# First half-FFN: ten pairs of the input phase by seven block products, modulation fetched one condition at a time in order of need, the context's operand at the memory's other end

## The chip, the core and the metric

The kernel runs on one core of a Trainium2 chip. The metric is the device time of one execution in microseconds (us); the profile is one execution recorded by the hardware profiler. Five engines matter: TensorE does the matmuls (PE; its weight loads, PEld, overlap them), VectorE (DVE) and ScalarE (ACT) prepare operands and finish results, GpSimd (POOL) does little here, and SyncE (SP) issues nearly all transfers, in order, on one queue. Each engine works through its own list of instructions in order; one that waits on a semaphore holds up everything behind it on that engine.

## The reference, cut to what matters

```python
def modulation(cond, w_mod, b_mod):
    m = jax.nn.silu(cond) @ w_mod + b_mod
    return m.reshape(m.shape[:-1] + (N_MOD, D_MODEL))          # 9 rows of 1024

def modulate(x, m, k):
    return x * (1 + m[..., 3 * k + 1, :]) + m[..., 3 * k, :]

def post_norm_update(x, y, m, k, g, b):
    return layer_norm(DN_ALPHA * x + m[..., 3 * k + 2, :] * y, g, b)

def swiglu(h, w_in, w_out):
    gate, up = jnp.split(h @ w_in, 2, axis=-1)
    return (jax.nn.silu(gate) * up) @ w_out

def macaron_half_ffn(x, m, k, w_in, w_out, g, b):
    return post_norm_update(x, 0.5 * swiglu(modulate(x, m, k), w_in, w_out), m, k, g, b)

# two layers; x is 512 tokens of 1024, ctx 256 tokens of 1024, the hidden width is 2816
for i in range(DEPTH):
    mx = modulation(c, mod_w[i], mod_b[i])
    x = macaron_half_ffn(x, mx, 0, ...)
    if ctx_needed:                                             # layer 0 only
        mc = modulation(c_ctx, mod_w[i], mod_b[i])
        ctx = macaron_half_ffn(ctx, mc, 0, ...)
    ...                                # mixer (HGRN2 or chunk MLP), then a second half-FFN
```

All of it is float32.

## The kernel before

**A product of float32 matrices** is made of three matmuls. Every operand is split into a high part (a rounded copy, by ACT, L135) and a low part (the difference, by DVE, L136), and `mm3` issues high times high, high times low and low times high (L148, L149, L150) into one PSUM bank. A *unit* is one weight tile of 128 x 1024 (512 KB): SP issues its load into `raw` (L141, a ring of three buffers), ACT writes the high half of `w` and DVE the low half (a ring of six), and PE uses it in eight steps of 128 rows.

**The first half-FFN on x** (`f0`, a `FeedIn`) needs gate and up for 22 hidden tiles, so 44 units in 22 *pairs*. The first three pairs (six units, `nu=6`) are fed while x arrives: for each of the eight row blocks k, DVE makes two columns of modulation (scale and shift) as dot products of rows of `mod_w` with the row silu(c), ACT applies them (L1014, L1019 for k = 0), the result is split into the operand `xm` (512 tokens), and `products` gives PE whatever that k allows. Then `rest(hp, 2)` (L590) does the other 19 pairs plainly: 2 units x 8 steps x 3 matmuls of 128x512, after which `evac` makes silu (ACT, L580) and h (DVE, L582). The out phase on x (`y`, 22 units of 24 matmuls of 128x512) follows, then the same weights once more for the 256 context tokens (`f1`, matmuls of 128x256, `psf<-xmc` in the rows), then the context's out phase. While `f1` runs, DVE and SP also finish x: the layer norm's last two steps (L338, L339) and the stores of x (L340).

**Modulation.** Beyond the two columns of the start, a `mod_task` makes one row of 1024: eight loads of 512 KB (`mraw`, two buffers, L176), each followed by dots with the silu row of one condition or of both (`x`, `c`). A dot is two instructions on halves of 512 (L170, each with its read of the accumulator) and, at the end of a row, a reduction joins the halves (L183). `mod_step(n)` takes the next n loads of the queue, with fractions saved up; it is called after each pair or unit. The queue holds: rows 2, 4, 3 for both conditions on one load, rows 1 and 0 for c, then 5, 7, 6, 8 and the next layer's row 2 for x: 80 loads and 104 dots.

**Seven products.** The second half-FFN of layer 0 and both of layer 1 already use another form of a pair (`seven`, of class `Forms`): gate and up together are a product of blocks, 2 x 2 blocks of the operand (halves of the 1024 rows, halves of the 512 tokens) by 2 x 2 blocks of the weights, done with seven block products in place of eight (Strassen-Winograd). The blocks of x are summed once (`sum_steps`: f5, f6, f7, f4); for every pair DVE makes three sums of weights (L660 to L663), so two loads become three and a half split weights. A pair is then 84 matmuls of 128x256 (`psc`, `pse`, `psa`). Its results leave through ACT (`sc`, L726) and DVE (L770 to L780).

**What sets the order.** The program names instructions in the order that one reads; a scheduler, with its own estimate of durations, then decides each engine's list, keeping what `issue_after` ties (a mod step behind the latest split). Buffers are tiles of pools: a tile that is used again makes the writer wait for its last reader.

**Memory.** The context's operand `xmc` (16 KB per partition, pool `xcp`) is taken from the start on the left side and kept until L1368, so the startup and `f0` do not have that space.

## Time and profile before

| | |
|---|---|
| three runs of the kernel | 2445.36, 2445.84, 2446.22 us; median 2445.84 |
| the profiled execution | 2444.88 us |
| its span in the profile | 2443.2 us |
| granted TensorE clock | 0.999 of full speed |

The stages, by the first and last starts of their matmuls in the trace:

| stage | us from the span's start | form of the matmuls |
|---|---|---|
| startup: three pairs while x arrives | 10.6 to 52 | 128x512 |
| 19 plain pairs of `f0` | 52 to 258 | 128x512 |
| out phase of x | 259 to 378 | 128x512 |
| input phase of the context, `f1` | 379 to 508 | 128x256 |
| out phase of the context, then HGRN2 | 508 to 1008 | mixed |
| second half-FFN of layer 0, input phase (seven products) | from 1009 | 128x256 |

How to read what follows: a row of the timeline is start, duration, engine, line, operation, what it writes and reads; the interval between the starts of two neighbours is what an instruction costs its engine, and that is often less than its duration, since neighbours overlap. A row of the windows gives, for a stretch of time, the busy time of each engine with its count, the granted clock, the mean share of the DMA engines in use and the bytes per second. "Idle before" and the arrow name what ended an engine's wait.

### The profile page before, as it was taken

How to read it: one execution, taken by the hardware profiler on the slowest of the kernel's cores; microseconds unless marked ns; L12 is line 12 of the kernel's file. 1: busy time of each engine (PE TensorE's matmuls, PEld its weight loads, DVE VectorE, ACT ScalarE, POOL GpSimd, SP SyncE). 2: the span in 40 equal slices, each digit the busy share in tenths (PEclk: the TensorE clock that was granted, in tenths of full speed). 3: DMA queues.
4: the chain of work that ended last, by engine and by line, in shares of the span. 5: the costliest groups of instructions: out<-in, count | busy, mean ns of one | idle time of the engine just before them, and what ended most of it. 6: DMA issues, size and time to landing. Idle time of an engine off the chain costs nothing.

```text
span 2443.2 us, 38143 instructions
## 1 busy us (share of the span) xinstructions
PE 2412.5 (99%) x14907; PEld 2186.0 (89%) x14907; DVE 1960.8 (80%) x3532; ACT 1151.1 (47%) x1784; POOL 35.2 (1%) x57
## 2 busy tenths in 40 slices
PE   7999999999999999999999999999999999999998
PEld 5888889988888888999988999988999988999987
DVE  7965679786488886988796988898898787988785
ACT  4222334454454452555643555544654443555641
POOL 0000000000000000000000000000000000000000
PEclk9999999999999999999999999999999999999999
DMA  8866555874212113433474333574322365333452
GB/s 325 296 207 203 164 177 193 297 245 162 67 48 65 61 48 113 160 104 106 147 235 151 104 104 104 163 248 154 115 86 99 116 226 170 130 114 104 139 163 79
DMA packets 107430, 366.01 MB, mean 150 GB/s; under 512 B 12473, under 2 KB 13809, under 8 KB 107249
## 3 DMA queue, kind: packets, MB, share of 16 engines
q1 hardware_dynamic: 107248, 363.58, 44.6%
q8 instruction: 116, 1.90, 0.3%
q14 instruction: 66, 0.53, 0.1%
HBM read 350.92 MB, written 12.61 MB: 149 GB/s over the span
## 4 chain that ended last, share of the span: by engine, by line
PE 89%; DVE 6%; ACT 3%; issue 1%; DMA 1%; POOL 0%; SPq 0%; DVEq 0%; POOLq 0%; ACTq 0%
PE y L148 10%; PE y L150 10%; PE y L149 10%; PE psf L150 5%; PE psf L149 5%; PE psf L148 5%; PE psc L148 5%; PE psc L150 5%; PE psc L149 5%; PE pse L150 3%; PE pse L148 3%; PE pse L149 3%; PE psa L150 1%; PE psa L149 1%; PE psa L148 1%; PE psq L148 1%
## 5 line engine op out<-in xcount | busy, mean ns | idle before, releaser
L136 DVE TENSOR_TENSOR w<-raw,w 128x1024 fp32r<-128x1024 f32 (+3 forms) x447 | 501.1, 1126 | 158.3 <-ACT w L135 157.4
L135 ACT ACTIVATE w<-raw 128x1024 fp32r<-128x1024 f32 (+3 forms) x447 | 436.1, 978 | 389.7 <-DMA raw<-in_ffn_w_in 71.4
L148 PE MATMUL y<-w,hs 128*128 128x512 f32 x984 | 383.7, 390 | 0.0
L150 PE MATMUL y<-w,hs 128*128 128x512 f32 x984 | 383.1, 389 | 0.0
L149 PE MATMUL y<-w,hs 128*128 128x512 f32 x984 | 382.9, 389 | 0.0
L135 ACT ACTIVATE hs<-h 128x512 fp32r<-128x512 f32 (+1 forms) x220 | 126.1, 587 | 202.1 <-PE y L150 180.4
L150 PEld LDWEIGHTS y<-w,hs 128*128 128x128 f32 x984 | 184.6, 188 | 39.7 <-DVE hs L136 1.3
L148 PEld LDWEIGHTS y<-w,hs 128*128 128x128 f32 x984 | 184.7, 188 | 38.6
L149 PEld LDWEIGHTS y<-w,hs 128*128 128x128 f32 x984 | 184.7, 188 | 37.8
L148 PE MATMUL psf<-xm,w 128*128 128x512 f32 (+1 forms) x544 | 191.3, 356 | 14.1 <-ACT xm L1019 10.6
L150 PE MATMUL psf<-xm,w 128*128 128x512 f32 (+1 forms) x544 | 192.2, 354 | 1.4 <-DVE w L136 1.4
L149 PE MATMUL psf<-xm,w 128*128 128x512 f32 (+1 forms) x544 | 192.1, 354 | 0.4 <-DVE xm L136 0.4
L136 DVE TENSOR_TENSOR hs<-h,hs 128x512 fp32r<-128x512 f32 (+1 forms) x220 | 135.3, 635 | 69.3 <-ACT hs L135 69.1
L148 PE MATMUL psc<-f,w 128*128 128x256 f32 x544 | 154.5, 284 | 1.1 <-ACT sc L726 1.1
L150 PE MATMUL pse<-f,w 128*128 128x256 f32 x544 | 154.2, 284 | 0.0
L148 PE MATMUL pse<-f,w 128*128 128x256 f32 x544 | 154.0, 283 | 0.0
L150 PE MATMUL psc<-f,w 128*128 128x256 f32 x544 | 153.9, 283 | 0.0
L149 PE MATMUL psc<-f,w 128*128 128x256 f32 x544 | 153.9, 283 | 0.0
L149 PE MATMUL pse<-f,w 128*128 128x256 f32 x544 | 153.9, 283 | 0.0
L148 PE MATMUL psc<-xm,w 128*128 128x256 f32 x532 | 151.5, 285 | 0.6 <-ACT sc L726 0.6
L150 PE MATMUL psc<-xm,w 128*128 128x256 f32 x532 | 150.5, 283 | 0.0
L149 PE MATMUL psc<-xm,w 128*128 128x256 f32 x532 | 150.5, 283 | 0.0
(342 smaller groups left out, 6013.0 us busy)
## 6 DMA issues: line engine op xcount, KB each, us to landing
raw<-in_ffn_w_in SPq DMA_DIRECT2D x159, 512.0 KB, 4.6
raw<-in_ffn_w_out SPq DMA_DIRECT2D x110, 512.0 KB, 4.2
mraw<-in_mod_w SPq DMA_DIRECT2D x80, 512.0 KB, 4.4
rawu<-in_mod_w SPq DMA_DIRECT2D x64, 512.0 KB, 4.0
rawu<-in_ffn_w_in SPq DMA_DIRECT2D x60, 512.0 KB, 3.6
x<-x SPq DMA_DIRECT2D x36, 512.0 KB, 4.4
raw<-in_hg_wf SPq DMA_DIRECT2D x32, 512.0 KB, 3.6
raw<-in_cm_w_out SPq DMA_DIRECT2D x24, 512.0 KB, 4.6
```

Of the source, the lines that this page charges most:

```text
L135: latest_hi[0] = nc.scalar.activation(dst_hi, src, AF.Copy)
L136: latest[0] = nc.vector.tensor_tensor(dst_lo, src, dst_hi.bitcast(F32), ALU.subtract)
L148: nc.tensor.matmul(ps, ah, bh, start=start, stop=False, **kw)
L149: nc.tensor.matmul(ps, ah, bl, start=False, stop=False, **kw)
L150: return nc.tensor.matmul(ps, al, bh, start=False, stop=stop, **kw)
```

## The change

Five things change.

1. `f0` becomes a `FeedSums` (still with six units in the startup). In the startup ACT also copies each modulated block of x into eight block tiles, two copies of 128x256 per k, that lie where later h tiles will be. `rest` does nine plain pairs first, one step of the sums in each of the first four, and then ten pairs by seven products.
2. A modulation row is made for one condition at a time, in order of need: 13 rows, so 104 loads of 512 KB in place of 80. The number of dots is the same. After a plain pair of `f0` 3.5 loads are taken, after a seven pair 0.5, after a unit of x's out phase 1.4 (1 before), after a pair of the context's input phase 1.4 (0.5 before).
3. A dot is one instruction over 1024 in place of two over 512, and the reduction goes. In the startup, where the accumulator has two columns, a dot is still two halves. The scratch output `junk` has one buffer in place of two.
4. `xcp` is allocated on the right side, after `f0` is done, and freed when the out phase of HGRN2 no longer needs it.
5. The modulation of the second layer, made in space cut from buffers of other stages (`Scraps`), takes one or two columns of accumulator, by the space that there is.

```diff
     def mod_dot(pool, dst, w, s):
-        n = D // 2
-        for i in range(2):
+        n = D // dst.shape[1]
+        for i in range(dst.shape[1]):
             c = slice(i * n, (i + 1) * n)
-            junk = pool.tile([P, n], BF16, tag="junk", name="junk", bufs=2)
+            junk = pool.tile([P, D // parts_of(pool)], BF16, tag="junk", name="junk", bufs=1)[:, :n]
             nc.vector.scalar_tensor_tensor(junk, w[:, c], 1.0, s[:, c], ALU.mult, ALU.mult, dst[:, i : i + 1])
+    def parts_of(pool):
+        return getattr(pool, "parts", 1)
     def mod_task(modp, srow, l, ch, conds):
-        accs = {c: modp.tile([P, KD, 2], F32, tag=f"acc_{c}", name=f"acc_{c}", bufs=2) for c in conds}
+        accs = {c: modp.tile([P, KD, parts_of(modp)], F32, tag=f"acc_{c}", name=f"acc_{c}", bufs=2) for c in conds}
...
-            dot = modp.tile([P, KD], F32, tag="dot", name="dot", bufs=2)
-            nc.vector.reduce_sum(dot, accs[c], axis=AX.X)
+            dot = accs[c][:, :, 0]
+            for i in range(1, parts_of(modp)):
+                nc.vector.tensor_tensor(dot, dot, accs[c][:, :, i], ALU.add)
...
-        def rest(self, hp, sp, nmod=0):
+        def rest(self, hp, sp, nmod=0, plain=0, nmod_plain=0):
...
-            for f in range(first, NF):
+            for f in range(first, first + plain):
+                self.plain_pair(hp, f)
+                with tc.issue_after(latest[0].ins):
+                    next(self.steps, None)
+                mod_step(nmod_plain)
+            for f in range(first + plain, NF):
...
-    xcp = L0.enter_context(sbuf(name="xcp", bufs=1))
-    xmc = new_xm(xcp, "xmc", TC)
...
-        f0 = FeedIn(0, 0, xm, NT, 6)
+        f0 = FeedSums(0, 0, xm, NT, lambda i: hp.tile([P, T], F32, tag="h", name="h", bufs=NF).rearrange("p (k t) -> p k t", k=2))
+        f0.nu = 6
...
+                for p in range(2):
+                    b = f0.blocks[p, k // 2] if k % 2 else f0.block(p, k // 2)
+                    nc.scalar.activation(b[:, k % 2, :], xf[:, p * 2 * P : (p + 1) * 2 * P], AF.Copy)
...
-        for ch in (2, 4, 3):
-            queue_mod(modp, srow, 0, ch, ["x", "c"])
-        for ch in (1, 0):
-            queue_mod(modp, srow, 0, ch, ["c"])
+        for ch, c in ((2, "x"), (1, "c"), (0, "c"), (4, "x"), (3, "x"), (2, "c"), (4, "c"), (3, "c")):
+            queue_mod(modp, srow, 0, ch, [c])
...
-        hget = f0.rest(hp, 2)
+        f0.enter()
+        f0.sums()
+        with sbuf(name="sp0", bufs=1) as sp:
+            hget = f0.rest(hp, sp, 0.5, 9, 3.5)
+        xcp = L0.enter_context(swap("xcp"))
+        xmc = new_xm(xcp, "xmc", TC)
...
-            ).run(bp, context_operand, 1)
-            hget = f1.rest(hp, 0.5)
+            ).run(bp, context_operand, 1.4)
+            hget = f1.rest(hp, 1.4)
...
-            op.release = late.close
+            def release():
+                late.close()
+                L0.close()
+            op.release = release
```

Three places show how the lists move; the words in brackets are the semaphores that an instruction waits for.

The first is ACT at the start of the program: `xm` is the operand's first block, `w` of 128x896 the rest of the first weight unit, on which the next matmuls wait. Before:

```order
L1019 ACTIVATE xm_88<-xt_115,cols_106 128x512 [waits DMAHW3_49,DVE_49]
L135 ACTIVATE w_133<-raw_132 128x896 [waits DMAHW0_49]
L135 ACTIVATE w_175<-raw_173 128x1024 [waits DMAHW4_49]
L1014 ACTIVATE xt_151<-xt_151,cols_106 128x512 [waits DMAHW2_49,DVE_49]
```

And of the change:

```order
L1032 ACTIVATE xm_88<-xt_111,cols_102 128x512 [waits DMAHW3_49,DVE_49]
L1039 ACTIVATE h_143<-xf_140 128x256 [waits DVE_49]
L1039 ACTIVATE h_145<-xf_140 128x256
L135 ACTIVATE w_129<-raw_128 128x896 [waits DMAHW0_49]
L135 ACTIVATE w_177<-raw_175 128x1024 [waits DMAHW4_49]
L1026 ACTIVATE xt_151<-xt_151,cols_102 128x512 [waits DMAHW2_49,DVE_49]
```

The two copies into block tiles now stand ahead of the weight's high half.

The second is DVE in the middle of the context's input phase, where `w` rows are the low halves of the next units, `h` the evacuation of a pair, `x` the layer norm's last steps and `junk` a dot of modulation. Before:

```order
L582 TENSOR_TENSOR h_3371<-psf_3344,silu_3369 128x256 [waits PE_49,Activation_49]
L136 TENSOR_TENSOR w_3413<-raw_3411,w_3413 128x1024 [waits DMAHW7_49]
L170 SCALAR_TENSOR_TENSOR junk_3447,acc_x_2942<-mraw_3445,srow_x_100 128x512 [waits DMAHW1_49]
L170 SCALAR_TENSOR_TENSOR junk_3449,acc_x_2942<-mraw_3445,srow_x_100 128x512
L338 SCALAR_TENSOR_TENSOR x_2070<-x_2070,rg_3374 128x512
L136 TENSOR_TENSOR w_3456<-raw_3454,w_3456 128x1024 [waits DMAHW0_49]
L339 SCALAR_TENSOR_TENSOR x_2070<-rb_3376,x_2070 128x512 [waits DVE_49]
L136 TENSOR_TENSOR w_3486<-raw_3484,w_3486 128x1024 [waits DMAHW2_49,Activation_49]
```

And of the change, from the unit at the same place on:

```order
L587 TENSOR_TENSOR h_3779<-psf_3752,silu_3777 128x256 [waits PE_49,Activation_49]
L344 SCALAR_TENSOR_TENSOR x_2489<-rb_3791,x_2489 128x512 [waits DVE_49]
L136 TENSOR_TENSOR w_3828<-raw_3826,w_3828 128x1024 [waits DMAHW4_49]
L170 SCALAR_TENSOR_TENSOR junk_3862,acc_x_3783<-mraw_3860,srow_x_96 128x1024 [waits DMAHW7_49]
L343 SCALAR_TENSOR_TENSOR x_2492<-x_2492,rg_3789 128x512
L170 SCALAR_TENSOR_TENSOR junk_3866,acc_x_3783<-mraw_3864,srow_x_96 128x1024 [waits DMAHW7_49,DVE_49]
L344 SCALAR_TENSOR_TENSOR x_2492<-rb_3791,x_2492 128x512 [waits DVE_49]
L587 TENSOR_TENSOR h_3858<-psf_3831,silu_3856 128x256 [waits PE_49,Activation_49]
L136 TENSOR_TENSOR w_3873<-raw_3871,w_3873 128x1024 [waits DMAHW5_49]
L136 TENSOR_TENSOR w_3903<-raw_3901,w_3903 128x1024 [waits DMAHW0_49,Activation_49]
```

Between the low halves of two units there stand two whole dots where there was one dot in halves, or none.

The third is PE at the same place of the change: `psf` are the banks of three units in a row.

```order
L148 MATMUL psf_3801<-xmc_2484,w_3798 128x256 [waits DVE_49,PE_49]
L149 MATMUL psf_3801<-xmc_2484,w_3798 128x256
L148 MATMUL psf_3831<-xmc_2484,w_3828 128x256 [waits DVE_49]
L149 MATMUL psf_3831<-xmc_2484,w_3828 128x256
L148 MATMUL psf_3876<-xmc_2484,w_3873 128x256 [waits DVE_49]
L149 MATMUL psf_3876<-xmc_2484,w_3873 128x256
L150 MATMUL psf_3801<-xmc_2484,w_3798 128x256 [waits DVE_49]
```

In the program before, the 24 matmuls of each of these units stand together; in the change, the first two of three units stand ahead of the 22 that need the first unit's low half.

More of the change, by code (lines that the diff above doesn't have):

```diff
@@ L201, in __init__ @@
         def __init__(self, pool, small, ring):
+            self.parts = D // small.shape[1]
             self.pool, self.small, self.ring, self.at, self.got = pool, small, ring, 0, {}
@@ L583, in evac, with plain_pair @@
             self.hs.append(h[:, :n])
+        def plain_pair(self, hp, f):
+            pss = []
+            for u in range(2):
+                w = unit(self.src(2 * f + u))
+                ps = bank("psf")
+                feat_mm(ps, w, self.xm, 0, self.n)
+                pss.append(ps)
+            self.evac(hp, *pss)
         def rest(self, hp, nmod):
@@ L588, in rest @@
             for f in range(len(self.hs), NF):
-                pss = []
-                for u in range(2):
-                    w = unit(self.src(2 * f + u))
-                    ps = bank("psf")
-                    feat_mm(ps, w, self.xm, 0, self.n)
-                    pss.append(ps)
-                self.evac(hp, *pss)
+                self.plain_pair(hp, f)
                 mod_step(nmod)
@@ L761, in rest @@
             N2, first = 2 * P, len(self.hs)
-            for f in range(first, NF):
+            for f in range(first, first + plain):
+                self.plain_pair(hp, f)
+                with tc.issue_after(latest[0].ins):
+                    next(self.steps, None)
+                mod_step(nmod_plain)
+            for f in range(first + plain, NF):
                 sc = sp.tile([P, 4, N2], F32, tag="sc", name="sc", bufs=2)
@@ L767, in rest @@
                     self.xm, sp, self.src(2 * f), self.src(2 * f + 1), [sc[:, i, :] for i in range(4)],
-                    self.steps if f == first else None,
+                    self.steps if f == first and not plain else None,
                 )
@@ L1015, in backbone_kernel @@
                     split(xm[:, 0, k, :], xm[:, 1, k, :], xt)
+                    xf = xt
                 else:
@@ L1365, in backbone_kernel @@
             f2.xm = op.xm = xm
-            op.release = late.close
+            def release():
+                late.close()
+                L0.close()
+            op.release = release
             op.run(bp)
-    L0.close()
     with sbuf(name="sp2", bufs=1) as sp, sbuf(name="hp2", bufs=1) as hp, bpools() as bp:
```

## The prediction

> **What bounds the kernel now.** I read the page's head first, then the waits on PE, then the windows by stage, then the timeline where a term needs a duration.
>
> ```profile
> span 2443.2 us, 38143 instructions
> PE 2412.5 (99%) x14907; PEld 2186.0 (89%) x14907; DVE 1960.8 (80%) x3532; ACT 1151.1 (47%) x1784; POOL 35.2 (1%) x57
> PE 89%; DVE 6%; ACT 3%; issue 1%; DMA 1%; POOL 0%; SPq 0%; DVEq 0%; POOLq 0%; ACTq 0%
> ```
>
> PE is busy nearly all the time and holds most of the chain that ends last. Busy time alone could hide a slow PE, so the waits come next: the three longest of the first 700 us, in which nearly all of the change lies.
>
> ```profile
> PE psf L148 <- ACT xm L1019: 10.6, 1, 10.6
> PE psf L148 <- ACT w L135: 3.0, 1, 3.0
> PE psf L150 <- DVE w L136: 1.0, 1, 1.0
> ```
>
> The columns are the sum, the count and the longest. Apart from the startup PE waits for almost nothing: fewer or shorter matmuls are worth their full interval, and any preparation that becomes late is paid in full. How near the helpers stand to that point is in the windows (span, then busy time of PE, PEld, DVE, ACT, POOL; clock; DMA share; GB/s).
>
> ```profile
> 12.00:24.00 12.00, 7.98 (x23) 5.24 (x22) 10.56 (x26) 6.43 (x8) 0.00 (x0) 1.00 1.03 419
> 60.00:100.00 40.00, 40.00 (x178) 33.14 (x177) 38.11 (x97) 11.63 (x13) 0.00 (x0) 1.00 0.90 313
> 400.00:420.00 20.00, 20.00 (x169) 20.00 (x168) 17.43 (x29) 7.57 (x12) 0.00 (x0) 1.00 0.84 277
> 420.00:440.00 20.00, 20.00 (x169) 20.00 (x168) 17.14 (x31) 9.04 (x11) 0.00 (x0) 1.00 0.89 291
> 460.00:480.00 20.00, 20.00 (x169) 20.00 (x168) 14.13 (x21) 9.68 (x12) 0.00 (x0) 1.00 0.88 302
> 1040.00:1140.00 100.00, 99.18 (x827) 98.98 (x826) 86.25 (x124) 57.02 (x99) 0.00 (x0) 1.00 0.32 106
> ```
>
> Three things are to be seen. In 12 to 24 us (startup) PE is starved and DVE full. In the plain pairs (60 to 100) DVE has little room. In the context's input phase (400 to 480) DVE leaves 2.6 to 5.9 us of every 20, at about 300 GB/s. The last row is a stage of seven products as `f0` will have it.
>
> **Term 1: ten pairs by seven products.** What a matmul costs is the interval of its starts.
>
> ```profile
> 32.52 0.39 PE L149 MATMUL psf<-xm,w 128*128 128x512 f32 x1
> ...
> 37.96 0.39 PE L150 MATMUL psf<-xm,w 128*128 128x512 f32 x1
> 408.08 0.28 PE L149 MATMUL psf<-xmc,w 128*128 128x256 f32 x1
> 408.20 0.28 PE L150 MATMUL psf<-xmc,w 128*128 128x256 f32 x1
> ```
>
> The first two rows are 24 matmuls of 512 apart: 5.44 / 24 = 0.2267 each. The other two are neighbours of 256: 0.12. A plain pair is 48 x 0.2267 = 10.88 us, a seven pair 84 x 0.120 = 10.08. Ten pairs save 10 x 0.80 = **8.0 us**, if helpers keep up. They do: by the row of 1040 to 1140 a seven pair takes DVE 86% of 10.08 = 8.7 us, half a dot adds 0.57 (below), sum 9.3 of 10.08. The dots' cover is thus 0.8 us a pair; beyond that every us is PE's.
>
> The Trainium skill, in "TensorE: Matmul & The Clock Gate", section "Back-to-back issue gap", speaks against it: sustained, a matmul of free size 128 takes about 81 ns and one of 512 about 131. Estimated from these, one of 256 takes 98 ns, a pair by seven 8.2 us against 6.3 plain, and ten pairs lose 19 us; the trace, with 0.12 and 0.2267, does not agree, and I go by it.
>
> **Term 2: the nine plain pairs.** What DVE's operations cost is again read from neighbours.
>
> ```profile
> 404.84 1.22 DVE L136 TENSOR_TENSOR w<-raw,w 128x1024 fp32r<-128x1024 f32 x1
> 405.98 0.42 DVE L582 TENSOR_TENSOR h<-psf,silu 128x256 f32<-128x256 f32 x1
> 406.31 0.68 DVE L338 SCALAR_TENSOR_TENSOR x<-x,rg 128x512 f32<-128x512 f32 x1
> 406.91 1.22 DVE L136 TENSOR_TENSOR w<-raw,w 128x1024 fp32r<-128x1024 f32 x1
> ...
> 410.81 0.69 DVE L170 SCALAR_TENSOR_TENSOR junk<-mraw,srow_x 128x512 bf16<-128x512 f32 x1
> ...
> 411.42 0.69 DVE L170 SCALAR_TENSOR_TENSOR junk<-mraw,srow_x 128x512 bf16<-128x512 f32 x1
> ```
>
> So 1024 wide costs 1.14, 512 wide 0.60, 256 wide 0.33, a dot's half 0.61, so a dot 1.22. A dot of 1024 in one is not in the trace: it lies between one half's 0.61 and 1.22, and I take 1.14, as the other two-operand form of that width. A plain pair in the change then costs DVE two splits (2.28), the evacuation (0.60), 3.5 dots (3.99) and, in the first four, the sums (two adds and two splits of 512: 2.40; the first pair has two adds more), together 9.3 of 10.88 us. Term 2 is **0**, hidden by 1.6 us a pair; the first weight sums for the seven pairs are made before PE ends the plain ones. The upper bound for an uneven order here is one pair's 1.6.
>
> **Term 3: the startup.** Two things are added: two copies of 128x256 per k on ACT, the first two ahead of the high half of `w`'s 896 columns; and, since `junk` has one buffer, each half of a dot now waits for the half before.
>
> ```profile
> 10.43 0.93 ACT L135 ACTIVATE w<-raw 128x896 fp32r<-128x896 f32 x1
> ...
> 2435.03 0.69 DVE L357 SCALAR_TENSOR_TENSOR t<-y,rgate 128x512 f32<-128x512 f32 x1 [0.21 <-PE y L150]
> 2435.75 0.69 DVE L359 TENSOR_TENSOR x<-x,t 128x512 f32<-128x512 f32 x1
> ```
>
> Where an operation needs its neighbour's result (2435.03 to 2435.75) the interval is 0.72 in place of 0.60: 0.12 more. DVE's low half stands behind ACT's 10.43 row, and the dots of k = 1 behind that, so the copies delay the chain by 2 x 0.33 = 0.67. For k = 1 and 2, while PE is still starved (8.0 of 12 us), three such waits each cost 2 x 0.36 = 0.72. Sum **+1.4 us**, between 0 (the chain rests on arriving weights, row of 3.0 above) and 3.2 (0.36 at each of seven k, plus 0.67). From 24 us on PE is continuous and absorbs the rest. A further **+0.5** (0 to 2.3, two dots) stands for the passage from the seven pairs to the out phase, where the first high and low halves of h must be ready at once.
>
> **Term 4: the context's input phase.** Here 1.4 dots a pair replace 0.5. DVE's groups in 392 to 442 (sum and mean, then idle before), and the landings in 396 to 510:
>
> ```profile
> L136 DVE TENSOR_TENSOR w<-raw,w 128x1024 fp32r<-128x1024 f32 x17 | 20.7, 1221 | 3.5 <-ACT w L135 3.5
> L339 DVE SCALAR_TENSOR_TENSOR x<-rb,x 128x512 f32<-128x512 f32 x8 | 5.5, 685 | 2.2 <-DMA rb<-in_ln_b 2.2
> L170 DVE SCALAR_TENSOR_TENSOR junk<-mraw,srow_x 128x512 bf16<-128x512 f32 x8 | 5.2, 686 | 0.0
> ...
> raw<-in_ffn_w_in SPq DMA_DIRECT2D x34, 512.0 KB, 4.8
> mraw<-in_mod_w SPq DMA_DIRECT2D x11, 512.0 KB, 5.8
> ```
>
> Eight halves are four dots, 4.9 us. In the change's list some eleven stand there: 12.5 us, so +7.6 against 5.7 us of idle time: at least **1.9 us** late. The order makes it more, since the dots stand ahead of the units that PE needs. Adding up DVE's new list at the intervals above, from the row where the first x step stood (391.67), gives the low half of the seventeenth unit at 431.5 us; PE would use it at its third matmul:
>
> ```profile
> 391.67 0.68 DVE L338 SCALAR_TENSOR_TENSOR x<-x,rg 128x512 f32<-128x512 f32 x1
> ...
> 428.36 0.28 PE L150 MATMUL psf<-xmc,w 128*128 128x256 f32 x1
> ```
>
> That is 3.2 us late; two units on the same again (437.3 for 434.1). By the unit of 440 the x steps are done and DVE catches up (row 460 to 480 has 5.9 of 20 free), so it is lost once. The new PE list adds to it: the first matmuls of the tenth and eleventh unit stand ahead of the ninth's 22, and their high halves need a `raw` whose buffer comes free with a low half at 402.5 (same sum): 402.5 + 4.8 + 1.06 (ACT's 0.93 for 896 columns, scaled to 1024) = 408.4, where DVE alone would have let the ninth go at 407.4. That is 1.0 more. Term 4 is **+4.2 us**, bounded by 1.9 below and, in rival (b), by 10 to 22 above.
>
> **The rest** is 0 with a bound of 1.5 either way: `xcp` on the other side changes which buffers the second half-FFN's tiles wait for, and some weight loads there trade places with stores; what PE waits there now is
>
> ```profile
> PE psc L148 <- ACT sc L726: 1.1, 2, 0.8
> ```
>
> One-pass dots elsewhere save DVE about 0.1 each, which PE does not feel.
>
> **Sum.** 2444.88 (the profiled execution) - 8.0 + 1.4 + 0.5 + 4.2 = 2443.0; the median of three runs lies 0.96 above that execution, so **2444.0 us**, 0.1% under 2445.84. That is inside 0.2% (4.9 us), about what a measurement of this kernel can tell from no change.
>
> **Rivals.** (a) **The gain stays whole**: the waits of term 4 are absorbed, because DVE is a unit ahead of PE now (the row of 406.91 ends at 408.13; it is the eleventh unit, needed at 428.36 - 6 x 2.88 = 411.08), or a one-pass dot is nearer 0.61 than 1.14. Then 2445.84 - 8.0 + 1.4 = 2439.2, with the startup free 2437.8. Against it: eleven dots at 1.14 overfill DVE even when packed.
>
> (b) **The modulation loads hold up the weights; slower.** `mraw` has two buffers and SP is in order, so a modulation load that waits for a buffer holds the weight load behind it. A load's turn is landing + dot + one split ahead of it: 5.8 + 1.14 + 1.14 = 8.1 us, for two buffers 4.04 each, while 1.4 per 5.76 us asks for one every 4.11. It decides from a landing of 5.95 us, just above today's. The new loads add 0.9 x 0.524 MB per 5.76 us = 82 GB/s to some 290. At a landing of 6.6 a pair takes 1.4 x 4.44 = 6.22 us, 22 pairs lose 10 in place of 4.2: 2449.8; at 7.4 (5.8 x 372/290) 6.78 and 22 in place of 4.2: 2462. For it: both loops are near full. Against it: 419 GB/s was reached in 12 to 24 us. The Trainium skill, "DMA: Bandwidth & Descriptors", section "Specifications", names a limit of about 358 GB/s from one core's share of memory; by it 372 GB/s over 127 us would cost 5 us more, but the startup's 419 does not agree.
>
> (c) **The startup loses more**, 3.2 in place of 1.4: 2445.8, still no change.
>
> (d) **Seven products gain nothing**, their pairs being bound by DVE at 10.9 us: 2452.0. The row of 1040 to 1140 speaks against it. From 10.88 / 84 = 0.130 us for a matmul of 256 they would lose outright; at 0.140 ten pairs would cost 8.8 more than plain ones, 2460.8 in all, but the rows have 0.120 throughout: 0.01 of the chance of (d).
>
> **How the numbers follow.** My forecast with (c), from 2441 to 2450.7: 0.54. (a): 0.26. (b) beyond 2450.7: 0.15. (d): 0.05. So faster by over 0.2%: 0.26; within: 0.54; slower: 0.20. The range reaches from 2438.5, inside (a), to 2452.5, which takes in (d) and the mild part of (b).
>
> **What would show it.** Starts of `psc` in `f0` 0.12 apart and pairs of 10.08 us confirm term 1. PE's first waits for `w` lengthening by about 1.4 us before 26 us confirm term 3. PE waits for DVE `w` (L136) and ACT `w` between 400 and 440 of 3 to 5 us, and none after 445, confirm term 4; waits spread to 508, with SP held on `mraw`, mean (b). A one-pass dot whose interval is far from 1.14, or a second half-FFN that starts otherwise by more than 1.5 us, would make me wrong.

## The result, and the profile after

| | before | changed |
|---|---|---|
| median | 2446.01 us (4 runs, 2445.36 to 2446.22) | 2459.95 us (4 runs, 2455.48 to 2462.80) |
| the profiled execution | 2444.88 | 2460.02 |
| ratio | | 1.0057, 95% interval 1.0045 to 1.0068 |

The change makes the kernel 0.57% slower, 13.9 us; 2444.0 us was predicted, in a range that ended at 2452.5. The runs of the changed kernel also lie 7 us apart where those of before lie within 1.

The head of the changed kernel's page (span, busy time by engine, chain by engine):

```profile
span 2458.3 us, 38793 instructions
PE 2413.8 (98%) x15267; PEld 2198.5 (89%) x15267; DVE 2009.9 (82%) x3315; ACT 1190.7 (48%) x1878; POOL 35.0 (1%) x57
PE 72%; DVE 13%; DMA 7%; ACT 4%; issue 3%; POOL 1%; SPq 0%; DVEq 0%; POOLq 0%; ACTq 0%
```

PE's busy time is as it was (2413.8 against 2412.5), though 8 us of matmul work are gone: a matmul counts as busy also where the granted clock was lower (0.83 in 400 to 410 us, below) or where its neighbour starts late but before its own row ends. The chain says more: PE's share fell from 89% to 72%, DVE's doubled and DMA, at 1% before, has 7%.

Where the time went is read from the starts of the first and last matmuls of each stage, in the profiled executions:

| stage | before | changed | difference |
|---|---|---|---|
| to the first matmul of x's out phase (startup and `f0`) | 258.76 | 254.48 | -4.3 |
| x's out phase | 119.82 | 121.28 | +1.5 |
| input phase of the context | 130.06 | 140.94 | +10.9 |
| from there to the second half-FFN (the context's out phase lies first in it) | 500.24 | 505.74 | +5.5 |
| from there to the last matmul | 1426.11 | 1427.70 | +1.6 |
| sum | | | +15.2 |

The gain of 4.3 us is there, and 16.4 us are given back in the context's input phase and the stage behind it. The changed kernel's windows there, in the columns of the prediction's rows:

```profile
400.00:420.00 20.00, 17.89 (x136) 17.41 (x134) 17.39 (x26) 6.53 (x9) 0.00 (x0) 0.91 0.87 289
420.00:440.00 20.00, 17.36 (x139) 16.52 (x137) 17.58 (x30) 7.40 (x9) 0.00 (x0) 1.00 0.96 332
460.00:480.00 20.00, 20.00 (x169) 20.00 (x168) 15.57 (x25) 8.30 (x12) 0.00 (x0) 1.00 0.90 309
```

PE has gaps, but DVE is no busier than before (17.4 and 17.6 of 20, 17.4 and 17.1 before). What has grown in the row of 420 is the DMA engines' share, 0.96 after 0.89, and the bytes. The landings of 396 to 510 us (count, KB each, median us from issue to landing) go with it for the weights: before they were 4.8 for the weights and 5.8 for the modulation loads, with 34 and 11 loads:

```profile
raw<-in_ffn_w_in SPq DMA_DIRECT2D x35, 512.0 KB, 5.6
mraw<-in_mod_w SPq DMA_DIRECT2D x25, 512.0 KB, 5.6
```

The chain through the first gap, in order of time (start, length, what):

```profile
398.75 1.15 DVE w L136
...
399.94 4.93 DMA raw<-in_ffn_w_in
...
404.90 1.07 ACT w L135
...
406.01 0.58 PE psf L148
406.59 0.22 PE psf L149
```

A low half frees a raw buffer at 399.9, the next weights take 4.93 us to land and 1.07 on ACT, and PE, whose list has these matmuls ahead of the 22 that it could do, waits. This is the place that term 4 described with its new PE list, 2.4 us earlier than there (406.0 for 408.4). But the same chain goes on with a landing of 6.64 us at 417.4, and from 477 on it is mostly landings of 5.6 to 8.5.

### The profile page after: what moved, and what is told of

It is laid out like the page before. It is cut to its first block, busy times and chain, and to the rows that moved or that the text cites. A ratio compares the mean times of both kernels' runs of the same rounds, so it can differ in the third digit from the quotient of the medians.

```text
span 2458.3 us, 38793 instructions
## 1 busy us (share of the span) xinstructions
PE 2413.8 (98%) x15267; PEld 2198.5 (89%) x15267; DVE 2009.9 (82%) x3315; ACT 1190.7 (48%) x1878; POOL 35.0 (1%) x57
## 4 chain that ended last, share of the span: by engine, by line
PE 72%; DVE 13%; DMA 7%; ACT 4%; issue 3%; POOL 1%; SPq 0%; DVEq 0%; POOLq 0%; ACTq 0%
PE y L150 7%; PE y L149 7%; PE y L148 7%; PE psc L148 6%; PE psc L150 6%; PE psc L149 6%; PE pse L150 3%; PE pse L148 3%; PE pse L149 3%; DVE w L136 3%; DMA mraw<-in_mod_w 3%; DMA raw<-in_ffn_w_out 2%; DVE junk L170 2%; ACT w L135 2%; DMA raw<-in_ffn_w_in 1%
## 5 line engine op out<-in xcount | busy, mean ns | idle before, releaser
L136 DVE TENSOR_TENSOR w<-raw,w 128x1024 fp32r<-128x1024 f32 (+3 forms) x447 | 495.2, 1113 | 142.8 <-ACT w L135 141.3
L148 PE MATMUL psc<-f,w 128*128 128x256 f32 x624 | 177.2, 284 | 1.6 <-ACT sc L734 1.5
L150 PE MATMUL pse<-f,w 128*128 128x256 f32 x624 | 176.9, 283 | 0.2 <-DVE w L136 0.2
L148 PE MATMUL pse<-f,w 128*128 128x256 f32 x624 | 176.7, 283 | 0.0
L150 PE MATMUL psc<-f,w 128*128 128x256 f32 x624 | 176.6, 283 | 0.0
L149 PE MATMUL pse<-f,w 128*128 128x256 f32 x624 | 176.6, 283 | 0.0
L149 PE MATMUL psc<-f,w 128*128 128x256 f32 x624 | 176.6, 283 | 0.0
L148 PE MATMUL psc<-xm,w 128*128 128x256 f32 x612 | 174.2, 285 | 0.9 <-ACT sc L734 0.9
L150 PE MATMUL psc<-xm,w 128*128 128x256 f32 x612 | 173.2, 283 | 0.0
L149 PE MATMUL psc<-xm,w 128*128 128x256 f32 x612 | 173.2, 283 | 0.0
L734 ACT ACTIVATE sc<-psc 128x256 f32<-128x256 f32 x218 | 83.5, 383 | 125.6 <-PE psc L150 119.6
L148 PE MATMUL psf<-xm,w 128*128 128x512 f32 (+1 forms) x384 | 127.4, 344 | 14.5 <-ACT xm L1032 11.1
L150 PE MATMUL psf<-xm,w 128*128 128x512 f32 (+1 forms) x384 | 130.4, 341 | 2.1 <-DVE w L136 2.1
```

The lines of the kernel that those rows point to most:

```text
L136: latest[0] = nc.vector.tensor_tensor(dst_lo, src, dst_hi.bitcast(F32), ALU.subtract)
L148: nc.tensor.matmul(ps, ah, bh, start=start, stop=False, **kw)
L149: nc.tensor.matmul(ps, ah, bl, start=False, stop=False, **kw)
L150: return nc.tensor.matmul(ps, al, bh, start=False, stop=stop, **kw)
L734: nc.scalar.activation(sc[i], ps[:, :N2], AF.Copy, scale=scale)
```

## The experiments

The first theory was that eleven dots overfill DVE (term 4 of the prediction). The rival: the loads behind them make the weights late, by their bytes, or by their place in the one queue and the turn of their two buffers. The stages of all runs, as above (us; medians and intervals of the ratio to before, which ran beside each):

| run | to x's out phase | x's out phase | context's input | to second half-FFN | rest | median | ratio (interval) |
|---|---|---|---|---|---|---|---|
| before | 258.8 | 119.8 | 130.1 | 500.2 | 1426.1 | | |
| changed | 254.5 | 121.3 | 140.9 | 505.7 | 1427.7 | 2459.95 | 1.0057 (1.0045, 1.0068) |
| x1_no_loads | 254.3 | 123.5 | 133.0 | 500.1 | 1427.4 | 2449.32 | 1.0015 (1.0006, 1.0024) |
| x2_no_dots | 254.2 | 122.0 | 137.3 | 503.0 | 1427.9 | 2452.60 | 1.0029 (1.0019, 1.0039) |
| s1_small_loads | 253.4 | 121.6 | 130.8 | 500.3 | 1427.6 | 2443.89 | 0.9994 (0.9985, 1.0003) |
| y4_before_late | 258.9 | 119.7 | 140.8 | 502.5 | 1425.8 | 2456.97 | 1.0051 (1.0036, 1.0066) |
| y1_pool_queue | 264.6 | 122.7 | 144.4 | 511.7 | 1434.4 | 2485.85 | 1.0169 (1.0149, 1.0190) |
| y2_ring3 | 253.2 | 119.9 | 138.1 | 503.3 | 1429.7 | 2452.39 | 1.0028 (1.0017, 1.0039) |
| y3_pool_ring3 | 256.7 | 119.9 | 144.3 | 510.0 | 1434.8 | 2473.54 | 1.0117 (1.0102, 1.0132) |
| z1_raw4 | 252.9 | 122.1 | 138.7 | 503.9 | 1428.8 | 2455.65 | 1.0041 (1.0027, 1.0054) |
| x3_half_rate | 253.1 | 135.3 | 132.3 | 506.6 | 1428.8 | 2469.19 | 1.0100 (1.0083, 1.0117) |
| x4_shared | 253.1 | 127.1 | 131.8 | 507.8 | 1427.1 | 2459.04 | 1.0056 (1.0041, 1.0071) |
| z2_ring3_early | 253.2 | 128.0 | 134.6 | 500.2 | 1428.6 | 2450.43 | 1.0020 (1.0011, 1.0029) |
| z4_start | 251.1 | 129.0 | 131.9 | 500.0 | 1429.7 | 2449.64 | 1.0017 (1.0008, 1.0026) |
| v1_spread | 251.0 | 122.0 | 131.4 | 500.6 | 1427.9 | 2446.03 | 1.0002 (0.9993, 1.0010) |
| v2_spread | 256.8 | 119.9 | 131.0 | 506.6 | 1427.3 | 2453.13 | 1.0034 (1.0021, 1.0047) |

### Dots without loads, loads without dots

The run x1_no_loads keeps the dots of the five last rows and leaves out their loads:

```diff
+            if (l, ch) in ((0, 5), (0, 7), (0, 6), (0, 8), (1, 2)) and len(srow) == 2:
+                raw = srow["x"]
+            else:
                 raw = modp.tile([P, D], F32, tag="mraw", name="mraw", bufs=2)
                 nc.sync.dma_start(raw, mod_w[l, ch, f])
```

> The changed kernel without the 40 loads of the five last modulation rows (those made from the end of x's out phase on); their dots stay, at full width, on the resident row silu(c) in place of the loaded rows, so these rows have other values. DVE's work is the same, 21 MB of transfers and their places in SP's queue are gone. Theory 1 (eleven dots overfill DVE in the context's input phase): the phase still lasts about 141 us and the time stays at 2456 us or more. Theory 2 (the modulation loads hold up the weight loads, by their place in the one queue, their two buffers and the bandwidth): the phase returns to some 130 to 133 us, its waits on DMA to what they were before, and the time falls to 2448 us or less.

The run x2_no_dots keeps the loads of these rows and makes their dots 8 columns wide:

```diff
-                mod_dot(modp, accs[c][:, f, :], raw, srow[c])
+                nc.vector.scalar_tensor_tensor(
+                    junk[:, :8], raw[:, :8], 1.0, srow[c][:, :8], ALU.mult, ALU.mult, accs[c][:, f, :])
```

> The changed kernel with the 40 loads of the five last modulation rows, but their dots only 8 columns wide, so these rows are not the reference's. The loads and their places in the queue are the same, and DVE loses some 1.05 us a dot, 30 dots in the context's input phase. Theory 1 (DVE overfull): the phase returns to 130 to 133 us, the time to 2448 us or less. Theory 2 (loads hold up the weights): the phase still lasts 137 us or more and the time stays at 2454 us or more; its dots release a buffer sooner, so a few us less than the changed kernel are possible.

The context's input phase took 133.0 us with the dots alone and 137.3 with the loads alone: 2.9 and 7.3 over before, 10.2 together where the change cost 10.9. The medians, 2449.3 and 2452.6, each miss their limit by about 1.4. So both theories hold a part, and the loads' is the larger. With the dots alone PE waits like this in 380 to 520 us:

```profile
PE psf L148 <- ACT w L135: 1.8, 1, 1.8
PE psf L150 <- DVE w L136: 0.5, 1, 0.5
```

The longer wait is at the ninth unit's place in PE's list, for a high half whose `raw` came free with a late low half; the shorter is for the low half of the seventh unit. The windows of the run with loads and narrow dots, its landings, and two landings on its chain:

```profile
400.00:420.00 20.00, 18.95 (x156) 18.55 (x155) 14.51 (x29) 6.19 (x9) 0.00 (x0) 1.00 0.92 322
420.00:440.00 20.00, 16.13 (x126) 15.08 (x125) 11.96 (x25) 7.01 (x8) 0.00 (x0) 1.00 0.84 283
```

```profile
raw<-in_ffn_w_in SPq DMA_DIRECT2D x34, 512.0 KB, 5.9
```

```profile
411.94 8.69 DMA raw<-in_ffn_w_in
...
421.60 6.84 DMA raw<-in_ffn_w_in
```

DVE is idle 8 of 20 us in the second row and PE has gaps all the same (busy 16.1 of 20): the weights land after 5.9 us, single ones after 8.7. After the phase the run without loads has lost nothing more (500.1), the run with them 2.7.

### Bytes, or places in the queue

The run s1_small_loads is x2_no_dots with the loads of these rows cut to 128 columns:

```diff
-            nc.sync.dma_start(raw, mod_w[l, ch, f])
+            nc.sync.dma_start(raw[:, :128], mod_w[l, ch, f][:, :128])
```

> The kernel of the run without full dots (40 late dots only 8 columns wide), and the 40 loads behind them cut to their first 128 columns (64 KB in place of 512), so these rows are not the reference's. The number of loads, their places in SP's queue and their waits for a buffer stay; seven eighths of their bytes go. If the loads cost by their bytes (they make weight loads land later), the context's input phase falls from the 137 us of that run to 132 or less and the time to 2446 us or less. If they cost by their place in the queue and the buffers' waits, the phase stays at 136 us or more and the time at 2450 or more.

It has the same loads at the same places in the queue, and an eighth of the bytes. Landings in 396 to 510 us, and all that PE waits for in 380 to 520:

```profile
raw<-in_ffn_w_in SPq DMA_DIRECT2D x34, 512.0 KB, 4.8
mraw<-in_mod_w SPq DMA_DIRECT2D x28, 64.0 KB, 3.7
```

```profile
PE psf L150 <- DVE w L136: 0.3, 1, 0.3
```

The phase is back at 130.8, the weights at 4.8 us, what follows at 500.3. SP's waits ahead of modulation loads shrank too, from 31.2 to 19.4 us in 380 to 517 (those for an earlier load's landing from 11.5 to 1.5); but the 19.4 that stay cost 0.7 us at most. With this the loads' part is shown to come from their bytes, and not from their number or places. Three runs that were made for the same question before say less: the run y1_pool_queue has the first edit, y2_ring3 the second, y3_pool_ring3 both.

```diff
-            nc.sync.dma_start(raw, mod_w[l, ch, f])
+            nc.gpsimd.dma_start(raw, mod_w[l, ch, f])
```

```diff
-            raw = modp.tile([P, D], F32, tag="mraw", name="mraw", bufs=2)
+            raw = modp.tile([P, D], F32, tag="mraw", name="mraw", bufs=3)
```

> The changed kernel with all modulation loads issued by GpSimd on its own queue in place of SyncE; nothing is left out. If a weight load is late because it stands behind a modulation load that waits for its buffer (SP waited 37.8 us for dots between 380 and 582 us of the changed kernel), SP's waits there go, the context's input phase falls from 141 to 134 us (the 133 of the run without these loads) and the time to 2452 us or less. If it is the bandwidth or the landing time that makes the weights late, the phase stays at 139 us or more and the time at 2457 or more.

> The changed kernel with three buffers for modulation loads in place of two; nothing is left out. If the round trip of a buffer (dot, then the queue, then some 5 us of landing, with DVE's next dot waiting in order) holds up the weights, three buffers free it: the context's input phase at 135 us or less, the time at 2452 us or less. If bandwidth does it, more loads in flight change nothing or make the weights land later: 2458 us or more.

> Both of the above: three buffers and GpSimd's queue. If order in the queue and the buffers' round trip are the cause, this is the fastest of the three, with only the dots' 3 us left in the context's input phase: 2444 to 2450 us. If bandwidth is the cause it is no better than the changed kernel, 2457 us or more.

The two runs with a queue of their own for these loads are worse, 144 us in the phase and 2 to 10 us more up to x's out phase. They are no clean test: the loads come at other times, and an issue occupies GpSimd for half a microsecond (group row of the page: busy, mean ns, idle before),

```profile
L179 POOL DMA_DIRECT2D mraw<-in_mod_w x104 | 55.3, 532 | 514.1 <-DVE junk L170 360.5 <-DVE h L789 78.5 <-DVE hs L136 22.9
```

and waits there for buffers, ahead of the layer norm's own work. A third buffer won some 7 us in all, but only 2.9 in the phase itself (138.1). SP's waits ahead of modulation loads fell there from 48.8 to 8.6 us (380 to 520), and 8.0 us of loss stayed, so the buffers' turn was a part of it, not the whole. The median landing of the weights in this run was 4.8 us, as before the change: a median over the phase does not show which landings PE waited for.

The run z1_raw4 gives every fourth raw weight of the context's input phase a buffer of its own:

```diff
+        if more[0] is not None and more[1] % 4 == 0:
+            raw = more[0].tile([P, 1024], F32, tag="raw4", name="raw", bufs=1)
+        else:
             raw = wpool.tile([P, 1024], F32, tag="raw", name="raw", bufs=3)
```

> The changed kernel with a fourth buffer for raw weights, in the context's input phase alone; nothing is left out and the rate stays at 1.4 loads a pair. Theory: weights are late there because a raw buffer's round (landing 5.6 us, ACT 1.06, DVE 1.2, and what SP holds) divided by three buffers exceeds the 2.88 us that PE needs a unit. A fourth buffer gives 11.5 us for a round in place of 8.6: the phase falls from 141 to 134 us or less (the dots' 3 us remain), the out phase after it starts with a lead, and the time falls to 2452 us or less. If bandwidth or DVE is the limit, a fourth buffer changes less than 2 us: 2457 or more.

Neither branch: it won 2.2 us in the phase, some 4 in all. The weights, with more of them in flight, landed after 6.2 us in place of 5.6:

```profile
raw<-in_ffn_w_in SPq DMA_DIRECT2D x34, 512.0 KB, 6.2
```

### The rate alone, in the kernel before

The run y4_before_late is the kernel before, with two rates moved:

```diff
-            ).run(bp, context_operand, 1)
-            hget = f1.rest(hp, 0.5)
+            ).run(bp, context_operand, 0.5)
+            hget = f1.rest(hp, 1.4)
```

> The kernel before, all 22 pairs plain or in the startup as they were, with only the rates of two stages moved: 0.5 modulation loads per unit of x's out phase (1 before) and 1.4 per pair of the context's input phase (0.5 before). Nothing is left out. If the rate in the context's phase alone makes the loss, without seven products, single-condition loads or the memory's order, that phase grows from 130 us to 136 to 141 and the time to 2451 to 2458 us. If the loss needs the other parts of the change, it stays within 3 us of before.

The phase takes 140.8 us, as in the changed kernel, with nothing else of the change in it. The rate is enough. Up to the second half-FFN it lost 2.3 us more, where the changed kernel lost 5.5.

Where in the phase the runs fall behind is read unit by unit: the start of a unit's last matmul, counted from the phase's first, less the same in the kernel before (us).

| run | unit 8 | 10 | 14 | 20 | 36 | 44 (last) |
|---|---|---|---|---|---|---|
| changed | 0.7 | 4.6 | 4.8 | 9.0 | 9.0 | 10.9 |
| x1_no_loads | 0.7 | 2.8 | 2.8 | 2.9 | 2.9 | 2.9 |
| x2_no_dots | 0 | 0 | 1.6 | 6.8 | 7.3 | 7.3 |
| s1_small_loads | 0 | 0 | 0 | 0.7 | 0.7 | 0.7 |
| y2_ring3 | 0.7 | 5.4 | 5.5 | 6.5 | 8.0 | 8.0 |
| z1_raw4 | 0.6 | 4.9 | 4.9 | 8.6 | 8.6 | 8.6 |
| y4_before_late | 0.8 | 0.8 | 2.1 | 10.6 | 10.6 | 10.7 |

The dots alone cost from the seventh to the ninth unit, the loads without full dots mostly from the eleventh to the twentieth, which the changed kernel ends at 445.7 us. From there to the thirty-sixth it loses nothing, though the loads go on at the same rate. The first stretch also has the end of the layer norm of x, whose stores are issued from 398.8 to 435.7 us. Whether these make the difference was not tried.

### The loads moved elsewhere

The run x3_half_rate moves the rates by the first edit; z2_ring3_early has it too, with three buffers and 0.6 in the context's out phase. The run x4_shared has the queue of before and the second edit.

```diff
-            ).run(bp, context_operand, 1.4)
-            hget = f1.rest(hp, 1.4)
+            ).run(bp, context_operand, 2)
+            hget = f1.rest(hp, 0.5)
```

```diff
-            hget = f0.rest(hp, sp, 0.5, 9, 3.5)
+            hget = f0.rest(hp, sp, 0.5, 9, 2)
...
-            hget = f1.rest(hp, 1.4)
+            hget = f1.rest(hp, 0.5)
```

> The changed kernel with 0.5 modulation loads per pair of the context's input phase, as before the change, and 2 in place of 1.4 per unit of x's out phase. Nothing is left out. Both theories have the context's input phase back at 130 us with no waits on PE; the context's out phase too should lose its 4.7 us if that loss came from starting without a lead. The front end's gain of 2.8 us at the start of the phase stays but for what two dots a unit cost in x's out phase (0 to 3 us). Time 2440 to 2446 us; over 2450 would mean that neither theory holds the cause.

> The changed kernel with the queue of before: rows 2, 4, 3 for both conditions on one load, 80 loads in place of 104, taken at 2 per plain pair, 0.5 per seven pair, 1.4 per unit of x's out phase and 0.5 per pair of the context's input phase. Nothing is left out. The dots are as many. If the context's rate and the 24 more loads are what cost, this keeps nearly all of the gain of the ten pairs: the context's input phase lasts 130 us and the time is 2439 to 2444 us. If the loss lies with the seven pairs themselves, the copies or the memory's new order, it stays above 2450 us.

> The changed kernel with three buffers for modulation loads and the loads moved out of the context's phase: 2 per unit of x's out phase, 0.5 per pair of the context's input phase, 0.6 per unit of its out phase. Nothing is left out. With two buffers x's out phase grew by 15 us at 2 loads a unit, because two loads took 6.1 us (landing 4.8 and two dots) where a unit takes 5.44; with three the round allows 2.4 a unit. Theory: x's out phase 120 to 122 us, the context's 130 to 132, what follows as before; time 2439 to 2443 us, faster than both kernels. If bandwidth is the limit, x's out phase grows by more than 5 us and the time stays above 2446.

In all three the context's input phase came back to 132 to 135 us, and none of them reached the kernel before: against the changed kernel x3_half_rate lost 9.2 us, x4_shared won 0.9 and z2_ring3_early 9.5. The first two lie above the 2450 us that their expectations took as the sign of another cause; the stages show that the cause in the context's phase went, and that time was lost where neither expectation had it. That is x's out phase, at one place near 320 us. The chain of the first shows the turn of the two buffers:

```profile
310.85 4.75 DMA mraw<-in_mod_w
...
315.69 1.23 DVE junk L170 x2
...
316.95 4.79 DMA mraw<-in_mod_w
...
321.84 1.23 DVE junk L170 x2
```

Two loads take 6.1 us from one to the next, a unit of PE 5.44; and since the dots stand in DVE's list ahead of the low halves of h, PE waits (`y` for `hs`, 10.7 us in five waits). Three buffers (z2) left one such wait of 6.1 us: there the context's operand, the layer norm of x's first half and the dots fill DVE together (10.00 of 10 us from 320), just behind a landing of the context's tokens of 4.11 us on the chain. The first and the shared loads have a second loss after the context's out phase, 4.3 to 4.5 us in which PE waits for the last modulation row (`pg` for `acc_x`): their rates leave the queue's last loads to that place.

### The startup

The run z4_start is z2_ring3_early with two scratch buffers for the startup's dots, and the two copies of each k behind that k's weights:

```diff
-            junk = pool.tile([P, D // parts_of(pool)], BF16, tag="junk", name="junk", bufs=1)[:, :n]
+            junk = (
+                pool.tile([P, n], BF16, tag="junk2", name="junk", bufs=2) if two else
+                pool.tile([P, D // parts_of(pool)], BF16, tag="junk", name="junk", bufs=1)[:, :n]
+            )
...
-                    nc.scalar.activation(b[:, k % 2, :], xf[:, p * 2 * P : (p + 1) * 2 * P], AF.Copy)
...
+                    with tc.issue_after(latest_hi[0].ins):
+                        nc.scalar.activation(b[:, k % 2, :], xf[:, p * 2 * P : (p + 1) * 2 * P], AF.Copy)
```

> The kernel of the run above, and in the startup the two parts undone that my prediction made responsible there: the scratch output of the dots has two buffers again, and the copies into block tiles stand behind the weights' high halves on ACT. Nothing is left out. If these two make the startup's loss (PE was 2.0 us later there), the first 50 us come back to within 0.7 us of before and the time falls by 1.3 to 2 us against the run above; if arriving weights make it, nothing changes.

The start of x's out phase moves from 253.2 to 251.1, by the 2 us that were expected; the median by 0.8 only, inside the spread of these runs. PE's waits for DVE in the first 60 us, changed kernel, then this run:

```profile
PE psf L150 <- DVE w L136: 1.7, 3, 0.9
```

```profile
PE psf L150 <- DVE w L136: 1.2, 1, 1.2
```

### All loads where there is room

The run v1_spread has three buffers, the startup of z4_start and these rates; v2_spread differs from it in them alone (0.9 and 4.3 in `f0`, 1.2, 0.65, 0.75):

```diff
-            hget = f0.rest(hp, sp, 0.5, 9, 3.5)
+            hget = f0.rest(hp, sp, 0.7, 9, 4)
...
-            ).run(bp, context_operand, 1.4)
-            hget = f1.rest(hp, 1.4)
+            ).run(bp, context_operand, 1.5)
+            hget = f1.rest(hp, 0.6)
...
-            ).run(bp, None, 0.5)
+            ).run(bp, None, 0.7)
```

> The changed kernel with three buffers for modulation loads, the startup of the run with the two parts undone, and the loads spread over the stages that have room: 4 per plain pair, 0.7 per seven pair, 1.5 per unit of x's out phase, 0.6 per pair of the context's input phase, 0.7 per unit of its out phase. Nothing is left out. From the stages of the other runs: start of x's out phase at 251 us (7.6 us ahead of before), that phase 120 to 122 us, the context's input phase 131 to 133, the rest as before: 2438 to 2442 us, faster than both kernels. If the loads cost wherever they are put, it stays above 2446.

> The kernel of the run with the loads spread, with still fewer in x's out phase, where that run lost 2.2 us at the place where the context's operand and the layer norm of x's first half fill DVE: 4.3 per plain pair, 0.9 per seven pair, 1.2 per unit of x's out phase, 0.65 per pair of the context's input phase, 0.75 per unit of its out phase. Nothing is left out. If that place is bound by DVE, x's out phase returns to 120 us, the profile's span to 2439 us and the median to 2440 to 2444 us, below both kernels. If the earlier stages have no room for the loads, the start of x's out phase moves from 251 to 253 us or later and nothing is won.

The first keeps 7.8 us up to x's out phase and loses 2.2 in it, 1.3 in the context's and 1.8 at the end. Its profiled execution is 2.2 us below that of before; its median over eleven runs, 2446.03 us from 2441.7 to 2450.8, is not: no change that can be measured, and the 2438 to 2442 expected were missed. The second has x's out phase back at 119.9, so that loss goes with the loads and dots taken there; which of the two it was, this run does not separate. But at 4.3 loads a plain pair the seven pairs begin without a lead and lose 5.9 us, and the context's out phase loses again. No version that computes everything beat the kernel before.

## Why the prediction was wrong

**Term 1 was right.** Pairs of `f0` by seven begin 10.08 us apart, to the hundredth:

```profile
172.40 0.28 PE L148 MATMUL psc<-xm,w 128*128 128x256 f32 x1
...
182.48 0.28 PE L148 MATMUL psc<-xm,w 128*128 128x256 f32 x1
```

Ten of them save the 8.0 us. The 0.5 us for a passage stood at the wrong end: from the last seven pair to the out phase it is 0.12 us in every run with seven pairs, while the first of the seven pairs lost 1.4 in the changed kernel and nothing in most others.

**Term 2 was right**: no gap in the plain pairs. So was the dot in one pass, taken as 1.14 us:

```profile
399.80 1.22 DVE L170 SCALAR_TENSOR_TENSOR junk<-mraw,srow_x 128x1024 bf16<-128x1024 f32 x1
400.94 0.08 DVE L170 DVE_READ_ACCUMULATOR junk<-mraw,srow_x 128x1 f32 x1
```

**Term 3** named two causes that together are right (the run with both undone wins 2.1 us; how much each makes was not tried) and was a little small, 1.4 for 2.0.

**Term 4 failed**, and with it the whole. The step that broke is "402.5 + 4.8 + 1.06": it adds weights that land in the 4.8 us of before, in a stage to which the same paragraph adds 0.9 loads a pair, and so puts what the loads do to the landing of the weights at nothing, without a reason. The loads without full dots cost 7.3 us in the phase; with an eighth of their bytes they cost 0.7. On the chain single weights landed after 6.64 us in the changed kernel, 8.69 and 6.84 without full dots.

The dots, priced at 3.2 and 1.0 us, cost 2.9 alone, and not where the sum has them. The 3.2 stand at the low half of the seventeenth unit, where the run with dots alone loses nothing; that they are near 2.9 is luck. It loses 0.7 at the seventh unit and 2.1 at the ninth, the latter by the path that the sum priced at 1.0: a late low half, then a landing (4.39 us there), then ACT.

How the bytes reach PE stays open. A raw buffer's round is landing, 1.06 on ACT, 1.14 to 1.22 on DVE and what it waits between; three buffers must bring a unit every 2.88 us, so 8.64 for a round. At 4.8 us that leaves 1.6 for waits, at 5.9 only 0.5. This sum makes it plausible that longer landings are felt, but it does not carry the whole: with one buffer more it leaves 3.1 at a landing of 6.2, and z1_raw4 still lost 8.6 us; and it would lose in every unit, where nothing was lost from the twentieth to the thirty-sixth.

The words "so it is lost once" hold for that stretch, but not for the whole. The last units lose 1.9 us more, and from the end of the input phase to the second half-FFN another 5.5 went. Without the bytes nothing did (500.1 and 500.3 against 500.2); the other runs with the bytes (x2, y2, y4, z1) lost 2.3 to 3.7 there. That it comes from a phase that ends without weights in advance is likely, and not shown.

By its own signs the prediction looked right: PE's waits for `w` between 400 and 440 came to 3.8 us, inside the 3 to 5 named for term 4. The loss is larger than these waits, since a row of a matmul is 0.28 us long where its neighbour could start after 0.12, so that a late start is counted only in part, and since the granted clock fell for a while (last section).

**Rival (b)** had the sign and, at its prices of 2449.8 to 2462, the size; it had 0.15. As a mechanism it was right in part: the bytes count. But its price rested on the modulation loads' own landing, which had to rise above 5.95 us and was 5.6; the turn of their buffers, which it named, is a part at most, since with a third buffer 8.0 of the 10.9 us stayed; and waits spread to 508, its sign, did not come. That its price fits is luck for the larger part. The reason given against it, 419 GB/s in the startup, was no reason: the weights came late in rows of 283 to 332 GB/s over 20 us, and x2_no_dots moved 404 from 410 to 415 us, near the startup's rate, in the very phase that loses. The Trainium skill, "DMA: Bandwidth & Descriptors", section "Specifications", names a limit of about 358 GB/s from one core's share of memory. These 5 us do not agree with it as a ceiling, and no row here shows that such a limit made the loss.

**The rest**, 0 with a bound of 1.5, was 1.6, just outside: every kernel with the changed memory takes 1.0 to 3.6 us longer from the second half-FFN on (leaving out the two on GpSimd's queue), the kernel before with moved rates does not (-0.3). Which wait makes it was not tried. Nor was the PE list, with two matmuls of three units ahead, tried by itself; the runs with and without dots differ in it too, so a part of the 2.9 us may be the list's.

## What to carry to other kernels

A load that is added to a stage costs more than the wait for itself. Before its price is added up, ask whether its bytes make the other loads of the stage land later, and do not take their landing from the trace without it. A stage where the consumer never waits may still have no room: before the change this phase ran without a gap at 0.84 to 0.89 of the DMA engines. And look at where in the stage the time is lost, unit by unit: a total can agree with a sum whose waits lie elsewhere.

## What was not expected of the hardware

After waits of 0.47 and 1.65 us between 403 and 406 us the matmuls of 256 ran 0.21 us apart in place of 0.12 for 2.9 us, some 1.3 us lost; the granted clock was 0.50 from 405.6 to 408.9. The windows of 400 to 410 us of the changed kernel, of the one with three buffers, and of the one without loads (granted clock third from the end):

```profile
400.00:410.00 10.00, 7.89 (x53) 7.48 (x52) 9.52 (x14) 2.81 (x4) 0.00 (x0) 0.83 0.96 317
```

```profile
400.00:410.00 10.00, 7.32 (x46) 6.92 (x45) 7.78 (x13) 3.83 (x6) 0.00 (x0) 0.83 0.95 322
```

```profile
400.00:410.00 10.00, 8.18 (x66) 7.97 (x67) 9.86 (x16) 3.23 (x5) 0.00 (x0) 1.00 0.63 205
```

The last has a wait of 1.8 us at the same place and kept the full clock. The Trainium skill, "TensorE: Matmul & The Clock Gate", section "HAM oscillation — how this bites in real kernels", puts the gap that matters at about 3.4 us; here shorter waits, close together, sometimes sufficed. What decides between them these runs do not show.
